# Two matmuls of 256 columns with the same weights become one of 512: the parts of x side by side

## The chip, the core and the metric

The kernel runs on one core of a Trainium2 chip. The engines of the core are named as in the profile: PE (TensorE, matmuls; PEld is its weight load), DVE (VectorE), ACT (ScalarE), POOL (GpSimd) and SP (SyncE, which issues most DMAs). The metric is the device time of one execution in microseconds.

## The reference

Two layers of a decoder on 256 tokens of width 2048, in float32. Layer 0 mixes by forgetting attention (8 heads of 128) beside a diagonal state-space part, layer 1 by sliding-window attention; each mixer is followed by a layer norm, and a gated feed-forward layer with a causal convolution of width 3 by another one.

```python
def _conv_ffn(x, w_up, conv_w, conv_b, w_down):
    s_len = x.shape[1]
    h = jnp.einsum('bsd,df->bsf', x, w_up)                 # 2048 -> 2 x 5504
    hp = jnp.pad(h, ((0, 0), (CONV_WIDTH - 1, 0), (0, 0)))
    h = conv_b + sum(conv_w[t] * hp[:, t:t + s_len] for t in range(CONV_WIDTH))
    gate = h[..., :D_FF]
    val = h[..., D_FF:]
    return jnp.einsum('bsf,fd->bsd', jax.nn.silu(gate) * val, w_down)
...
    proj = jnp.einsum('bsd,de->bse', x, w_in)              # layer 0: q, k, v, forget gate, u
    z = jnp.einsum('bsc,ce->bse', jax.nn.gelu(y.reshape(bsz, s_len, SSM_WIDTH)), w_glu)
    ssm = z[..., :SSM_WIDTH] * jax.nn.sigmoid(z[..., SSM_WIDTH:])
```

## The kernel before

Every float32 operand of a large product is split into two float32r parts, hi (ACT rounds it, L110 for weights) and lo (DVE subtracts, L115), and a product w x is built of three: hi(w) hi(x), hi(w) lo(x) and lo(w) hi(x). All matmuls go through `mm` (L234).

The weights stream through the kernel once, in the order of their use, in chunks of 512 KB (128 partitions x 1024 columns): `Stream` loads a chunk by SP into one of five raw buffers, splits it into one of four pairs of rotating buffers (tiles `hi` and `lo` in the profile) and hands it over. `done()` after a chunk frees its buffers, splits further chunks as far as three are held, and then pumps the side generators: each emits one step of other work (state-space vectors, an attention head, a finished column of the feed-forward layer). The order of all instructions on every engine is that in which this code emits them.

There are two shapes of product. In `amm` the stationary operand is 128 tokens of a transposed activation and 512 weight columns move: the result is natural, [token, feature]. It serves v, the output projections, the down projections and all of layer 1's mixer. In `bmm` the stationary operand is a 128 x 128 block of the weights, and the 256 tokens of the transposed x move: the result is [feature, token]. `xT[:, k]` holds k-tile k as [128, 2, 256], the hi part in index 0 of the second axis, the lo part in index 1. `bmm` serves u (the input of the state-space part, 8 tiles of 16 k-tiles), the forget gate, q and k of 8 heads (`b_tile`), the GLU, and columns 2 to 42 of both up projections, where a column j is a pair of 128 features, one of the gate and one of the value (`up_chunk`, four chunks to a pair). These are 3152 k-tiles, each with three matmuls into the first 256 columns of a PSUM bank of 512.

What reads the banks: ACT copies u to the tile `ut`, which goes through memory to the state-space part; ACT copies q (scaled) and k to the tiles `qk`, and one pump later the head's first product of q and k stands on PE. For the GLU, ACT takes the sigmoid of one bank and DVE multiplies it by the other. For the feed-forward layer `finish_gen` does ACT's scaling with bias from the bank, one pump later four DVE convolution steps from the bank, then silu and product, then the split into `act`.

Around a layer norm, `boundary` transposes x four tiles at a time (`turn`), through a scratch tile `x32`, by lists of steps (`PLAN_TAIL`, `PLAN_MID`, `PLAN_HEAD`).

Of the kernel before, what the change touches and what calls it, by code (L numbers as in the profile page):

```python
# [21 lines left out]
P = 128  # L22
T = 256
# [22 lines left out]
# around a layer norm, after each chunk: s split the next chunk (s0, s1: with the statistics of that half  # L46
# of the tokens in between), n normalize, t transpose, l second parts; digits: half, quarter of the columns
# [9 lines left out]
class Stream:  # L57
    """Weights in the order of use: DMA, split into two float32r parts, hand over. The parts of an item
    go to a rotating buffer, or to where its dst says: a function that gives (hi, lo), or None as long
    as there is no room."""  # L60
# [28 lines left out]
    def split_next(self, steps=None, late=False):  # L89
        """steps: a serial chain of short vector instructions to put in between; late: give back the  # L90
        function that does the second part"""
# [77 lines left out]
    def get(self):  # L169
        """The next chunk's parts; free() or done() must follow each, in order, after its last use."""  # L170
        while self.split <= self.pos:
            assert self.room(self.split, 0)
            self.split_next()
        o = self.outs.pop(self.pos)
        self.pos += 1
        return o
# [24 lines left out]
def trunk(ctx: ExitStack, tc: tile.TileContext, A, out):  # L201
# [39 lines left out]
    def k_exp(o, x, t, tk, ti):  # L241
        """o = exp(x); t, tk float scratch, ti int32 scratch. Yields the time of what it emitted."""
# [18 lines left out]
    def k_sincos(s, c, x, t, tk):  # L261
        """s, c = sin(x), cos(x)."""
# [28 lines left out]
    def gmul(o_re, o_im, a, b, t1, t2):  # L291
        """cmul on GpSimd, for the small tables it has time for"""
# [5 lines left out]
    def cmul(o_re, o_im, a, b, t1, t2):  # L298
        """(o_re, o_im) = a * b, complex; a, b are (re, im) pairs, the outputs no inputs."""
        mul(t1, a[0], b[0])  # L300
        mul(t2, a[1], b[1])
        sub(o_re, t1, t2)
        mul(t1, a[0], b[1])
        mul(t2, a[1], b[0])
        add(o_im, t1, t2)

# [26 lines left out]
    def ext(place, c):  # L333
        """the last four of the eight chunks on either side of a layer norm"""
# [71 lines left out]
    def warm(f):  # L406
        """the table of f, ahead of its first use"""
        S.activation(spare, spare, f)

# [1 line left out]
    def bmm(ps, hi, lo, k, first, last, src=None):  # L411
        """ps[f, t] += w[k, f] x[k, t]"""
        s = xT if src is None else src
        mm(ps, hi, s[:, k, 0, :], first, False)
        mm(ps, hi, s[:, k, 1, :], False, False)
        mm(ps, lo, s[:, k, 0, :], False, last)

    def amm(o, hi, lo, src, k, tb, first, last):
        """o[t, f] += x[k, t] w[k, f] for one half of the tokens"""
# [5 lines left out]
    def a_chunk(part, o, src, k, tb, first, last, n=2):  # L425
        """One chunk of the stream: n k-tiles of 512 columns."""
# [29 lines left out]
    def ln_stats(tb):  # L456
        """mean in lnw[:, tb, 0], 1 / sqrt(var + eps) in lnw[:, tb, 2], one short step at a time"""
# [20 lines left out]
    def four_places(t_, a=0):  # L478
        """room for the parts of four chunks in t_ [P, n, 2, T]"""
# [4 lines left out]
    def boundary(li, tail, resid, after_tail, head):  # L484
        """The last eight chunks of a product, the layer norm, the first eight chunks of the next
        product, each for one half of the tokens after the other: the norm of one half runs under the
        products of the other."""
        with tc.tile_pool(name="lnp", bufs=1) as lp:
# [5 lines left out]
            def turn(tb, q):  # L494
# [3 lines left out]
                x32 = mk(lp, [P, 4, P], tag="x32", bufs=3)  # L498
# [56 lines left out]
    def affine_gen(li, pool):  # L555
        """Gain and bias on the natural x, which only the next residual needs."""
# [18 lines left out]
    class Ffn:  # L575
# [13 lines left out]
        def up_chunk(self, part, c):  # L589
            hi, lo = part  # L590
            for kk in range(4):
                k = 4 * c + kk
                for e in range(2):
                    sl = slice(kk * T + e * P, kk * T + e * P + P)
                    bmm(self.ps[e][:, :T], hi[:, sl], lo[:, sl], k, k == 0, k == KT - 1)

        def head(self, part, tb, c):
            """columns 0 and 1 of the up projection, natural"""
# [17 lines left out]
        def finish(self, j):  # L616
            """convolution, gate and split of column j, among the next chunks"""
            self.gens.append(st.add(self.finish_gen(j, self.ps), 0.1))

        def finish_gen(self, j, ps):  # L620
            cw, y = self.cw, []
            for e in range(2):
# [17 lines left out]
        def run(self, li):  # L640
            """Everything but the last four chunks of the down projection."""
# [36 lines left out]
    def final(ffn, li):  # L678
        """The last layer norm, to the output."""
# [33 lines left out]
    def rope_gen(rp):  # L713
        """cos and sin of the rotary angles, and the sinks"""
# [12 lines left out]
    def apply_rope(t_, nh, rt_):  # L727
        """t_ [P, 2, nh, 64], in place on the first 16"""
# [166 lines left out]
    # =================================================================  # L895
    # layer 0, mixer
    # =================================================================
    cell = {}

    def s5_gen(p, wk, u4):  # L900
        """State-space part, everything but the u projection. Yields the vector work it emitted, in us;
        0 leaves the rest to the next call, for what waits on another engine."""
# [32 lines left out]
        def phasors():  # L935
            """Powers 0..7 of w = (cs + i sn)^4, in pb, and of w^8, in pa."""
# [65 lines left out]
        def tab(dst, sc, src, b):  # L1002
            """dst = sc * src, complex, in blocks on the diagonal of each pair of groups"""
# [577 lines left out]
```

## Time and profile before

| | before |
|---|---|
| median of 3 runs | 2156.82 us (2156.72 to 2157.05) |
| the profiled execution: its span | 2155.2 us |
| beside the span, to the median of the runs | 1.6 us |
| PE busy | 2123.6 us (99%), 14236 matmuls |
| DVE busy | 1380.7 us (64%) |
| ACT busy | 1056.6 us (49%) |
| DMA | 389.22 MB, mean 181 GB/s |

Busy time of PE is time in which at least one matmul is under way; durations of neighbouring matmuls overlap, so the distance between their starts, and not their duration, says how many fit into a stretch. The layer 0 mixer lasts until about 400 us, the feed-forward layer of layer 0 until about 1150 us, the mixer of layer 1 until about 1410 us, and the second feed-forward layer to the end.

### The profile page before, as it was taken

The numbers are of one execution on the slowest core, as the hardware profiler recorded it, in microseconds if no ns is written. First come the engines' busy times: TensorE is split into PE (matmuls) and PEld (weight loads), VectorE is DVE, ScalarE is ACT, GpSimd is POOL, SyncE is SP. The second block draws the span as 40 slices with busy tenths as digits, with TensorE's granted clock in tenths as the row PEclk, the third lists the DMA queues.
The fourth block names the chain that finished last, engine by engine and source line by source line (L and its number), as shares of the span: only waits on it lengthen the run. The fifth ranks groups of instructions, "written<-read, shape, count | busy, mean of one in ns | idle before, by whom it ended". The sixth has DMA issues, their size and how long they took to land.

```text
span 2155.2 us, 35663 instructions
## 1 busy us (share of the span) xinstructions
PE 2123.6 (99%) x14236; PEld 1934.8 (90%) x14236; DVE 1380.7 (64%) x2120; ACT 1056.6 (49%) x1586; POOL 78.1 (4%) x143
## 2 busy tenths in 40 slices
PE   8999999999999999999999999999999999999997
PEld 8899989799999999988887877889999999988886
DVE  7898856786566566544456876767656656654445
ACT  5445544655555455433336665465555545543332
POOL 4600000000000000000001000000000000000000
PEclk9999999999999999999999999999999999999999
DMA  8554456575665665656664644656665566656654
GB/s 289 153 168 130 128 193 203 163 217 185 186 182 181 186 184 180 186 183 187 190 200 147 186 127 127 205 160 210 183 186 182 181 186 185 179 186 189 189 183 160
DMA packets 111478, 389.22 MB, mean 181 GB/s; under 512 B 13072, under 2 KB 15120, under 8 KB 111056
## 3 DMA queue, kind: packets, MB, share of 16 engines
q1 hardware_dynamic: 104112, 371.37, 55.3%
q10 hardware_dynamic: 5712, 10.20, 1.7%
q0 software_dynamic: 1488, 5.38, 0.8%
q8 instruction: 112, 1.84, 0.3%
q14 instruction: 54, 0.44, 0.1%
HBM read 383.75 MB, written 3.15 MB: 180 GB/s over the span
## 4 chain that ended last, share of the span: by engine, by line
PE 96%; DVE 3%; ACT 1%; issue 1%; DMA 0%; DVEq 0%; ACTq 0%
PE bank L234 94%; DVE t L231 0%; DVE t L213 0%; PE bank L497 0%; DVE t L115 0%; DVE t L228 0%; PE bank L820 0%; PE bank L1031 0%; DVE z L213 0%; DVE lo L115 0%; ACT x L501 0%; DVE t L127 0%; DMA raw<-wu 0%; PE bank L823 0%; PE bank L779 0%
## 5 line engine op out<-in xcount | busy, mean ns | idle before, releaser
L115 DVE TENSOR_TENSOR lo<-raw,hi 128x1024 fp32r<-128x1024 f32 (+1 forms) x674 | 818.9, 1218 | 652.5 <-ACT hi L110 650.6
L234 PE MATMUL bank<-t,hi 128*128 128x256 f32 x6304 | 1140.2, 284 | 6.8 <-ACT t L110 6.0
L110 ACT CAST hi<-raw 128x1024 fp32r<-128x1024 f32 x677 | 705.7, 1045 | 688.1 <-PE bank L234 570.1
L234 PEld LDWEIGHTS bank<-t,hi 128*128 128x128 f32 x6304 | 985.1, 192 | 8.4 <-ACT t L110 6.0
L234 PE MATMUL bank<-t,lo 128*128 128x256 f32 x3152 | 893.0, 283 | 0.0
L234 PE MATMUL bank<-hi,t 128*128 128x512 f32 x2248 | 720.8, 397 | 0.0
L234 PEld LDWEIGHTS bank<-t,lo 128*128 128x128 f32 x3152 | 606.0, 192 | 0.1
L234 PEld LDWEIGHTS bank<-hi,t 128*128 128x128 f32 x2248 | 423.0, 188 | 102.2 <-issue 3.8
L234 PE MATMUL bank<-lo,t 128*128 128x512 f32 x1124 | 443.8, 395 | 0.4 <-DVE lo L115 0.4
L234 PEld LDWEIGHTS bank<-lo,t 128*128 128x128 f32 x1124 | 211.7, 188 | 49.5 <-DVE lo L115 1.3
L625 ACT ACTIVATE y<-bank,t 128x256 f32<-128x256 f32 x172 | 87.9, 562 | 134.1 <-PE bank L234 127.4
L231 DVE SCALAR_TENSOR_TENSOR y<-bank,t,y 128x255 f32<-128x255 f32 (+1 forms) x344 | 141.6, 475 | 1.9 <-ACT y L625 1.9
L234 PE MATMUL bank<-t,t 128*128 128x512 f32 (+3 forms) x422 | 89.6, 357 | 9.6 <-DVE t L115 7.8
L234 PEld LDWEIGHTS bank<-t,t 128*128 128x128 f32 (+1 forms) x422 | 63.0, 177 | 23.0 <-DVE t L115 8.8
L634 ACT ACTIVATE y<-y 128x256 f32<-128x256 f32 x86 | 35.9, 418 | 31.9 <-DVE y L231 31.9
L804 ACT ACTIVATE p<-bank,sm 128x128 f32<-128x128 f32 (+1 forms) x64 | 26.1, 420 | 45.2 <-DVE sm L213 45.2
L501 ACT ACTIVATE x<-bank,t 128x128 f32<-128x128 f32 x96 | 36.1, 457 | 19.5 <-PE bank L497 19.4
L213 DVE TENSOR_TENSOR t<-y,t 128x256 fp32r<-128x256 f32 x86 | 35.9, 419 | 0.9 <-ACT t L237 0.9
L213 DVE TENSOR_TENSOR y<-y,y 128x256 f32<-128x256 f32 x86 | 35.9, 420 | 0.3 <-ACT y L634 0.3
L237 ACT CAST t<-y 128x256 fp32r<-128x256 f32 x86 | 34.5, 402 | 3.3 <-DVE y L213 3.2
L213 DVE TENSOR_TENSOR t<-t,gbn 128x1024 f32<-128x1024 f32 x24 | 29.3, 1222 | 10.2 <-DMA gbn<-ln 10.2
L213 DVE TENSOR_TENSOR t<-bank,t 128x256 fp32r<-128x256 f32 (+3 forms) x34 | 17.6, 524 | 24.5 <-ACT t L237 24.4
(163 smaller groups left out, 899.0 us busy)
## 6 DMA issues: line engine op xcount, KB each, us to landing
raw<-wup SPq DMA_DIRECT2D x328, 512.0 KB, 3.6
raw<-wdn SPq DMA_DIRECT2D x168, 512.0 KB, 3.6
raw<-wo SPq DMA_DIRECT2D x64, 512.0 KB, 3.6
raw<-wi SPq DMA_DIRECT2D x40, 512.0 KB, 3.7
raw<-wqk SPq DMA_DIRECT2D x32, 512.0 KB, 3.6
raw<-wu SPq DMA_DIRECT2D x16, 512.0 KB, 5.5
raw<-wv SPq DMA_DIRECT2D x16, 512.0 KB, 3.7
raw<-wg SPq DMA_DIRECT2D x16, 512.0 KB, 4.0
```

Of the source, the lines that this page charges most:

```text
L110: self.nc.scalar.copy(hi, r)
L115: eng.tensor_tensor(lo, r, hi.bitcast(F32), op=ALU.subtract)
L213: V.tensor_tensor(o, a, b, op=op)
L231: V.scalar_tensor_tensor(o, a, s, b, op0=op0, op1=op1)
L234: PE.matmul(o, lhsT=l, rhs=r, start=start, stop=stop)
L237: S.copy(hi, src)
L501: S.activation(x32[:, j], pt[:, j * P:(j + 1) * P], AF.Identity, bias=lnT[:, li, 1, k:k + 1], scale=lnT[:, li, 0, k:k + 1])
L625: S.activation(y[e], ps[e][:, :T], AF.Identity, bias=cw[:, n, 3:4], scale=cw[:, n, 2:3])
L634: S.activation(y[0], y[0], AF.Silu)
L804: S.activation(pp[:, e], vv[:, e], AF.Exp, bias=sm[:, 0, qb, e:e + 1], scale=1.0, accum_out=sm[:, 2, qb, e:e + 1])
```

## The change

`bmm` issues two matmuls instead of three. The hi part of the weights multiplies both parts of the transposed x, 512 columns, into the whole bank: hi(w) hi(x) lands in columns 0 to 255, hi(w) lo(x) in 256 to 511. The lo part of the weights multiplies the hi part of x, 256 columns, into columns 256 to 511. Whoever reads the bank adds the halves: `joined` copies the second half out of PSUM on ACT and adds the first on DVE. The q tile is scaled by ACT on the way and added by one scaled step of DVE; the GLU joins both of its banks ahead of the sigmoid; `finish_gen` joins both banks of a pair into new tiles `h0` and `h1` one pump ahead of its old first step. Columns 0 and 1 of each up projection, which come from `amm`, are not joined. The scratch tile `x32` has two buffers instead of three. Comments are taken out, so line numbers move.

```diff
-    def bmm(ps, hi, lo, k, first, last, src=None):
-        s = xT if src is None else src
-        mm(ps, hi, s[:, k, 0, :], first, False)
-        mm(ps, hi, s[:, k, 1, :], False, False)
-        mm(ps, lo, s[:, k, 0, :], False, last)
+    def bmm(ps, hi, lo, k, first, last):
+        mm(ps, hi, xT[:, k].rearrange("p a t -> p (a t)"), first, False)
+        mm(ps[:, T:], lo, xT[:, k, 0, :], False, last)
+
+    def joined(o, ps, view=lambda a: a):
+        S.copy(o, view(ps[:, T:]))
+        add(o, o, view(ps[:, :T]))
...
-                x32 = mk(lp, [P, 4, P], tag="x32", bufs=3)
+                x32 = mk(lp, [P, 4, P], tag="x32", bufs=2)
...
-                    bmm(self.ps[e][:, :T], hi[:, sl], lo[:, sl], k, k == 0, k == KT - 1)
+                    bmm(self.ps[e], hi[:, sl], lo[:, sl], k, k == 0, k == KT - 1)
...
-            self.gens.append(st.add(self.finish_gen(j, self.ps), 0.1))
+            self.gens.append(st.add(self.finish_gen(j, self.ps, j >= 2), 0.1))
...
-        def finish_gen(self, j, ps):
+        def finish_gen(self, j, ps, halves):
             cw, y = self.cw, []
+            if halves:
+                h = [mk(self.w, [P, T], tag=f"h{e}", bufs=1) for e in range(2)]
+                for e in range(2):
+                    joined(h[e], ps[e])
+                ps = h
+                yield 0
...
-                    S.copy(ut, o.rearrange("p (n l) -> p l n", l=LCH))
+                    joined(ut, o, lambda a: a.rearrange("p (n l) -> p l n", l=LCH))
...
-    S.copy(ft, ps[0:8, :T])
+    joined(ft, ps[0:8])
...
             if j == 0:
-                S.mul(t_, ps[:, :T], 1.0 / math.sqrt(128.0))
+                c = 1.0 / math.sqrt(128.0)
+                S.mul(t_, ps[:, T:], c)
+                stt(t_, ps[:, :T], c, t_, ALU.mult, ALU.add)
             else:
-                S.copy(t_, ps[:, :T])
+                joined(t_, ps)
...
-        S.activation(sg, zz[1][:, :T], AF.Sigmoid)
-        mul(sg, sg, zz[0][:, :T])
+        joined(zl, zz[0])
+        joined(sg, zz[1])
+        S.activation(sg, sg, AF.Sigmoid)
+        mul(sg, sg, zl)
```

On PE the triples become pairs at every place alike. In an up projection (`t_77` is xT, the banks are those of a column pair) these rows stand before the change, where "x2" is two matmuls with the same weights, one after the other:

```order
L234 MATMUL bank_5771<-t_77,hi_5729 128x256 x2
L234 MATMUL bank_5771<-t_77,lo_5730 128x256
L234 MATMUL bank_5772<-t_77,hi_5729 128x256 x2
L234 MATMUL bank_5772<-t_77,lo_5730 128x256
L234 MATMUL bank_5771<-t_77,hi_5761 128x256 x2
```

and at the same place with the change:

```order
L234 MATMUL bank_5122<-t_77,hi_5084 128x512
L234 MATMUL bank_5122<-t_77,lo_5085 128x256
L234 MATMUL bank_5123<-t_77,hi_5084 128x512
L234 MATMUL bank_5123<-t_77,lo_5085 128x256
L234 MATMUL bank_5122<-t_77,hi_5108 128x512
```

The order of tiles and chunks is the same; the two matmuls with a hi block have become one of twice the columns.

On ACT, one column pair of an up projection, from the cast of the pair before (`t_4533`, after the change `t_4070`, is `act`) to the next cast of this kind; before:

```order
L237 CAST t_4533<-y_392_5329 128x256
L110 CAST hi_5470<-raw_5292 128x1024
L625 ACTIVATE y_400_5476<-bank_5332,t_4534 128x256
L625 ACTIVATE y_401_5478<-bank_5333,t_4534 128x256
L110 CAST hi_5511<-raw_5325 128x1024
L110 CAST hi_5549<-raw_5362 128x1024
L634 ACTIVATE y_400_5476<-y_400_5476 128x256
L110 CAST hi_5585<-raw_5403 128x1024
```

and with the change:

```order
L237 CAST t_4070<-y_421_4914 128x256
L418 COPY h_422_5008<-bank_4888 128x256
L418 COPY h_423_5009<-bank_4889 128x256
L110 CAST hi_5032<-raw_4873 128x1024
L634 ACTIVATE y_426_5038<-h_422_5008,t_4071 128x256
L634 ACTIVATE y_427_5040<-h_423_5009,t_4071 128x256
L110 CAST hi_5058<-raw_4910 128x1024
L110 CAST hi_5084<-raw_4940 128x1024
L643 ACTIVATE y_426_5038<-y_426_5038 128x256
L110 CAST hi_5108<-raw_4970 128x1024
L237 CAST t_4070<-y_427_5040 128x256
```

The copies are new; they now stand where PE's last matmul of the pair is waited for, and the activations come a chunk later and read the joined tiles.

On DVE, in the stretch of q and k of the fifth head (`z` and `ph` are state-space vectors, `fsm` and `fp` the head before), with the change:

```order
L213 TENSOR_TENSOR z_216_2210<-bank_2140,ph_1944 128x512
L231 SCALAR_TENSOR_TENSOR qk_220_2215<-bank_2105,qk_220_2215 128x256
L115 TENSOR_TENSOR lo_2236<-raw_1971,hi_2235 128x1024
...
L115 TENSOR_TENSOR lo_2264<-raw_2029,hi_2263 128x1024
L213 TENSOR_TENSOR z_216_2210<-z_216_2210,z_217_2211 128x512
L213 TENSOR_TENSOR z_218_2212<-z_218_2212,z_219_2213 128x512
L1136 SCALAR_TENSOR_TENSOR z_217_2211<-t_200,z_216_2210 128x512
L213 TENSOR_TENSOR qk_224_2278<-qk_224_2278,bank_2218 128x256
L115 TENSOR_TENSOR lo_2299<-raw_2086,hi_2298 128x1024
```

Before, DVE had no instruction that wrote q or k (tile `qk`). The step for q now stands behind one product of the state-space part, the one for k behind its first scan.

## Rows read from the trace of the kernel before

**Rows 1.** The page: span, busy time by engine, and the chain that ended last.
```profile
span 2155.2 us, 35663 instructions
PE 2123.6 (99%) x14236; PEld 1934.8 (90%) x14236; DVE 1380.7 (64%) x2120; ACT 1056.6 (49%) x1586; POOL 78.1 (4%) x143
...
PE 96%; DVE 3%; ACT 1%; issue 1%; DMA 0%; DVEq 0%; ACTq 0%
PE bank L234 94%; DVE t L231 0%; DVE t L213 0%; PE bank L497 0%; DVE t L115 0%; DVE t L228 0%; PE bank L820 0%; PE bank L1031 0%; DVE z L213 0%; DVE lo L115 0%; ACT x L501 0%; DVE t L127 0%; DMA raw<-wu 0%; PE bank L823 0%; PE bank L779 0%
```

**Rows 2.** Waits of PE, the two largest: us in total, times, longest.
```profile
PE bank L234 <- DVE t L115: 8.6, 4, 2.7
PE bank L234 <- ACT t L110: 6.0, 1, 6.0
```

**Rows 3.** Groups by shape of PE, whole span: busy us, mean ns of one.
```profile
L234 PE MATMUL bank<-t,hi 128*128 128x256 f32 x6304 | 1140.2, 284 | 6.8 <-ACT t L110 6.0 <-DVE t L115 0.8
L234 PE MATMUL bank<-t,lo 128*128 128x256 f32 x3152 | 893.0, 283 | 0.0
```

**Rows 4.** Windows, up projection: length, busy PE, PEld, DVE, ACT, POOL; clock, DMA.
```profile
600.00:700.00 100.00, 100.00 (x836) 100.00 (x835) 61.52 (x88) 50.63 (x70) 0.00 (x0) 1.00 0.60 184
```

**Rows 5.** Timeline of PE, up projection: start, length, merged matmuls.
```profile
800.12 0.40 PE L234 MATMUL bank<-t,hi 128*128 128x256 f32 x2
...
811.64 0.40 PE L234 MATMUL bank<-t,hi 128*128 128x256 f32 x2
```

**Rows 6.** Timeline of PE, output projection of layer 0, state-space half.
```profile
365.14 0.61 PE L234 MATMUL bank<-hi,t 128*128 128x512 f32 x2
...
372.62 0.61 PE L234 MATMUL bank<-hi,t 128*128 128x512 f32 x2
```

**Rows 7.** Timeline of PE, down projection of the first feed-forward layer.
```profile
904.20 0.63 PE L234 MATMUL bank<-hi,t 128*128 128x512 f32 x2
...
911.23 0.63 PE L234 MATMUL bank<-hi,t 128*128 128x512 f32 x2
```

**Rows 8.** Timeline of PE, scores of layer 1's attention (moving operand: its keys).
```profile
1203.15 0.51 PE L234 MATMUL bank<-t,qT 128*128 128x256 f32 x3
1203.50 0.28 PE L234 MATMUL bank<-t,t 128*128 128x256 f32 x1
1203.62 0.86 PE L234 MATMUL bank<-t,qT 128*128 128x512 f32 x3
1204.32 0.40 PE L234 MATMUL bank<-t,t 128*128 128x512 f32 x1
```

**Rows 9.** Groups by shape of ACT up to 440 us: the copy of k.
```profile
L1386 ACT COPY qk<-bank 128x256 f32<-128x256 f32 x8 | 3.1, 384 | 1.0 <-PE bank L234 1.0
```

**Rows 10.** Groups by shape of DVE up to 440 us: a product and a scaled step.
```profile
L213 DVE TENSOR_TENSOR sg<-sg,bank 128x256 f32<-128x256 f32 x8 | 3.4, 419 | 4.9 <-ACT sg L1432 4.9
L231 DVE SCALAR_TENSOR_TENSOR y<-bank,t,y 128x255 f32<-128x255 f32 x4 | 1.7, 476 | 0.0
```

**Rows 11.** Waits from 480 to 1000 us, the largest entry.
```profile
DVE lo L115 <- ACT hi L110: 208.3, 140, 2.5
```

**Rows 12.** Windows, 20 us in the stretch of q and k (columns as in rows 4).
```profile
200.00:220.00 20.00, 20.00 (x166) 19.84 (x165) 19.60 (x30) 9.30 (x18) 0.00 (x0) 1.00 0.51 148
```

**Rows 13.** Timelines of DVE and PE there: what precedes the products of heads five and six.
```profile
204.20 1.22 DVE L1127 TENSOR_TENSOR_SCAN z<-t,z 128x512 f32<-128x512 f32 x1
217.47 1.89 DVE L213 TENSOR_TENSOR z<-t,bt 128x512 f32<-128x512 f32 x3
...
206.20 0.39 PE L234 MATMUL bank<-qk,qk 128*128 128x128 f32 x2
219.80 0.39 PE L234 MATMUL bank<-qk,qk 128*128 128x128 f32 x2
```

**Rows 14.** Timeline of ACT, a sigmoid of the GLU with the idle time before it.
```profile
341.84 0.39 ACT L1432 ACTIVATE sg<-bank 128x256 f32<-128x256 f32 x1 [1.96 <-PE bank L234]
```

**Rows 15.** Timeline of PE, its second matmul of all.
```profile
7.36 0.58 PE L234 MATMUL bank<-t,hi 128*128 128x256 f32 x1 [0.76 <-DVE t L115]
```

More of the change, by code (lines that the diff above doesn't have):

```diff
@@ L1338, in trunk @@
                     st.get()
-                o = ps[i - i0][:, :T]
+                o = ps[i - i0]
                 for j in range(8):
@@ L1359, in trunk @@
     for k in range(KT):
-        bmm(ps[:, :T], hi[:, 8 * k:8 * k + P], lo[:, 8 * k:8 * k + P], k, k == 0, k == KT - 1)
+        bmm(ps, hi[:, 8 * k:8 * k + P], lo[:, 8 * k:8 * k + P], k, k == 0, k == KT - 1)
     st.done()
     ft = mk(fp, [8, T])
-    S.copy(ft, ps[0:8, :T])
+    joined(ft, ps[0:8])
     gate = st.add(fox_gate(ft, fp))
@@ L1380, in trunk @@
             ps = bank(acc)
-            b_tile(ps[:, :T], 2)
+            b_tile(ps, 2)
             t_ = mk(fp, [P, T], tag=f"qk{j}", bufs=2)
             if j == 0:
-                S.mul(t_, ps[:, :T], 1.0 / math.sqrt(128.0))
+                c = 1.0 / math.sqrt(128.0)
+                S.mul(t_, ps[:, T:], c)
+                stt(t_, ps[:, :T], c, t_, ALU.mult, ALU.add)
             else:
-                S.copy(t_, ps[:, :T])
+                joined(t_, ps)
             qk.append(t_)
@@ L1421, in trunk @@
             for k in ks:
-                bmm(z[c][:, :T], hi[:, k * P:(k + 1) * P], lo[:, k * P:(k + 1) * P], k, k == 0, k == 7)
+                bmm(z[c], hi[:, k * P:(k + 1) * P], lo[:, k * P:(k + 1) * P], k, k == 0, k == 7)
     for c in range(4):
@@ L1428, in trunk @@
             for j in range(2):
-                b_tile(z[j][:, :T], 1)
+                b_tile(z[j], 1)
         sg = mk(gp, [P, T], tag="sg")
+        zl = mk(gp, [P, T], tag="zl")
         zz = z[2 * i:2 * i + 2] if i < 2 else z
-        S.activation(sg, zz[1][:, :T], AF.Sigmoid)
-        mul(sg, sg, zz[0][:, :T])
+        joined(zl, zz[0])
+        joined(sg, zz[1])
+        S.activation(sg, sg, AF.Sigmoid)
+        mul(sg, sg, zl)
         split_to(xT[:, 8 + i, 0, :], xT[:, 8 + i, 1, :], sg)
```

## The prediction

> **What bounds the kernel now.** I read the page's head and its chain of waits first: PE is busy 2123.6 us of a span of 2155.2 us, and the chain that ended last runs through PE for 96% of the span, 94% on the matmul line L234 [rows 1]. Then the waits of PE: the two largest entries come to 8.6 and 6.0 us in five waits [rows 2], so there is next to no idle time to win; what counts is how long a matmul holds PE. The groups by shape name what the change touches: 6304 matmuls of 256 columns with the hi part of a weight as stationary operand and 3152 with the lo part [rows 3], that is 3152 triples hi, hi, lo. The windows say what the other engines do meanwhile: in the first up projection PE is busy without a gap, DVE 62% and ACT 51% of the time [rows 4].
>
> The number that matters is the pitch, the distance from start to start, for a duration in these rows holds latency that the next matmul overlaps. In the up projection 32 triples go from 800.12 to 811.64 us: 0.360 us each, 0.120 us per matmul of 256 columns [rows 5]. For 512 columns there are two paces. In the output projection of layer 0, where the operands are x^T and the rotating weight parts, 11 triples take 7.48 us: 0.680 us each, 0.2267 us per matmul [rows 6]. In the down projection, with the activations as one operand, 10 triples take 7.03 us: 0.703 us, 0.2343 us per matmul [rows 7]. Products of layer 1's attention give 0.2333 us (three in 0.70 us), and four matmuls of 256 columns just ahead of them 0.47 us, 0.1175 us each [rows 8].
>
> **The change, part by part.** *PE.* Each triple of 256 columns becomes one matmul of 512 and one of 256; the columns stay 768. The clock was granted in full there, the 2.4 GHz level [rows 4]. From 256 to 512 columns the faster pace grows by 0.1067 us, which is 256 periods of that clock: a column costs one period. Taken off, 0.0133 us per matmul is left at 256 columns [rows 5] as at 512 in the faster pace [rows 6], and 0.021 us in the slower [rows 7]. This fixed part is what a merged pair pays once instead of twice. For the 512 I take 0.2267, because there the operands lie in the same two buffers as in the merged product, x^T and the rotating parts, with the roles exchanged; the other end is 0.2343. For the 256 behind it I keep 0.120; the other end is 0.1175. The new pair is then 0.3467 us and saves 13.3 ns; the ends are 15.8 and 5.7 ns. Some ten triples run at the start before the clock is up, so 3140 x 13.3 ns = 41.9 us saved (ends 50 and 18 us).
>
> Here a rule of the notes speaks against the change. The Trainium skill, TensorE: Matmul & The Clock Gate, section "Back-to-back issue gap", puts the isolated pitch at N/2.4 + 2.5 ns, so that merging would save 2.5 ns, 7.9 us in all. The trace does not agree with its constant: its fixed part is 13 to 21 ns.
>
> *Feed-forward layers, 41 column pairs each.* Each pair gets two ACT copies out of PSUM (0.384 us each by the like copy of k) [rows 9] and two DVE additions with a PSUM operand (0.419 us) [rows 10]: 0.77 us of ACT and 0.84 us of DVE for a PE time of 32 x 0.3467 = 11.1 us. DVE goes from 0.62 x 11.52 = 7.1 us to 7.9 us, 72%; ACT from 5.8 to 6.6 us, 60%. I cost this at nothing: DVE's idle time there is a wait for the next cast (208.3 of 520 us) [rows 11], and the cast waits for a weight buffer that PE still reads, so splits run up to three chunks (8 us) ahead. If that cover went, the bare price is 2 x (0.384 + 0.419) = 1.6 us per pair. The banks come free at the join, two pumps earlier than the four convolution steps let them go; the convolution starts one pump later, and only the last pair of a layer could feel it, whose rows the down projection reads last in each of its column blocks. The later steps read SBUF instead of PSUM; I keep their price.
>
> *u, q and k, layer 0.* Here DVE also carries the state-space vectors: 19.60 us busy of 20 from 200 us on [rows 12]. Added: 8 joins of u, one of the gate, and for each of 8 heads a q step (0.476 us, as the like step) and a k step (0.419 us) [rows 10]: 9 x 0.419 + 8 x 0.895 = 10.9 us. Until now q and k needed ACT alone; now the head's product waits for DVE's queue. For the fifth head the k step stands behind the scan that starts at 204.20 and lasts 1.22 us, so it ends at 205.84, before the product at 206.20. For the sixth it stands behind three products from 217.47 to 219.36, ends at 219.78 or, pushed by the two steps before it less 0.4 us of slack, at 220.3: after the product's old start of 219.80 [rows 13]. So about 0.5 us at the worst heads, less where DVE has gaps. u's additions fall into chunks in which DVE waits for a cast anyway. I take 3 us for this stage (ends 0 and 10.9). The u vectors reach memory some 0.5 us later, long before they are used.
>
> *GLU.* Each pass gets two more copies and additions ahead of its sigmoid: copy, copy, addition, about 1.2 us longer, where ACT was idle 1.96 us before the sigmoid [rows 14]. Hidden, except for the first two passes, which come together: 0.5 us (ends 0 and 2.4).
>
> *Start.* The first matmul now needs both parts of x. PE ran one matmul early and then waited 0.76 us for the lo part [rows 15]; that early one is lost: 0.3 us, at most its 0.58 us.
>
> *x32 with two buffers instead of three.* Each transposition at a layer norm then needs the second part of the one two before it; the plan has that subtraction emitted by then in every case. Nothing; a late one would cost one subtraction, some 0.7 us, at three norms.
>
> Sum: -41.9 + 3 + 0.5 + 0.3 = -38.1 us on the span of 2155.2 us. The median of the runs, 2156.8 us, lies 1.6 us above the span; so 2118.7, given as **2119 us** (-1.8%).
>
> **The rivals.** (B) The merged matmul goes at the slower pace, 0.2343 us: 5.7 ns per triple, 17.9 us, less 3.8 us of costs: 2142.7 us. For it: most 512-column matmuls of this kernel run so, and I know no cause of the two paces. Against: the stretch with the operands in the same two buffers has the faster one throughout.
>
> (C) Columns are all that counts: the 512 takes as long as the two it replaces, 0.240 us. Nothing is saved and 3.8 us are added: 2160.6 us. It decides from 0.2388 us on (3.8 us / 3140 = 1.2 ns). Against it: no stretch that I read has more than 0.2343. By the page's constant named above, the same case ends at 2152.7 us.
>
> (D) Slower: the joins stop the queues of ACT and DVE in the up projection. The copy waits for PE to end its column; behind it stand the casts, behind the addition the subtractions of the next chunks. If the lead of three chunks is used up, each pair shows up to 1.6 us: 82 x 1.6 = 131 us, so up to 2118.7 + 131 = 2250 us. It turns the gain into a loss from 0.43 us per pair on (32 x 13.3 ns). For it: the addition now makes DVE wait for PE's last matmul of a pair, through ACT. Against it: ACT's old first step waited for that same matmul, and PE had no gap in that window [rows 4].
>
> **How the numbers follow.** My forecast 0.62, with a range of its own of 2108 to 2128 us (15.8 ns and costs near nothing; costs of 13 us); B 0.20; C 0.09; D 0.09. About 0.2%, 4.3 us, is what a measurement of this kernel can tell from no change. My forecast and B are faster by more: 0.82, and 0.01 of C joins them; 0.08 of C is within that bound, with 0.01 of D; 0.08 is slower. The range 2108 to 2147 us takes in my case and B with its costs up to 8 us, and leaves out C, D and the tails.
>
> **What would show it.** Right: PE with 3152 hi matmuls of 512 columns and as many lo of 256; pair pitch 0.347 us in the up projections and no PE gap there, DVE near 72% and ACT near 60%; an up projection shorter by 17.5 us a layer (41 x 0.427); a few PE waits on DVE, of up to 1 us, at the heads between 120 and 240 us. Wrong: a pair pitch of 0.354 (B) or 0.36 (C); PE waits on the subtraction of L115 or the cast of L110 between 450 and 900 us (D); DVE waits of several us ahead of each head's product, which would make the layer 0 mixer eat the gain.

## The result and the profile after

| | before | after |
|---|---|---|
| median of 4 runs each, same chip | 2156.94 us (2156.72 to 2157.28) | 2135.20 us (2134.24 to 2136.38) |
| ratio after to before | | 0.9902, 95% interval 0.9888 to 0.9916 |
| span of the profiled execution | 2155.2 us | 2134.0 us |

The change makes the kernel faster by 1.0%: 21.2 us of span, where 38.1 us were forecast. The head of the page and the chain that ended last, after:

```profile
span 2134.0 us, 29675 instructions
PE 2089.1 (98%) x11084; PEld 1759.7 (82%) x11084; DVE 1464.5 (69%) x2325; ACT 1110.9 (52%) x1766; POOL 74.7 (3%) x143
...
PE 90%; DVE 6%; ACT 2%; DMA 1%; issue 1%; POOL 0%; SPq 0%; ACTq 0%; DVEq 0%; POOLq 0%
```

PE has 3152 matmuls fewer and is busy for 34.5 us less, but the span fell by 21.2 us only: the chain, 96% PE before [rows 1], is now 90% PE and 6% DVE. The pace in an up projection is not the reason. PE's timeline there (start, length), 16 merged pairs from the first row to the last:

```profile
799.99 0.40 PE L234 MATMUL bank<-t,hi 128*128 128x512 f32 x1
800.22 0.28 PE L234 MATMUL bank<-t,lo 128*128 128x256 f32 x1
800.34 0.39 PE L234 MATMUL bank<-t,hi 128*128 128x512 f32 x1
...
805.53 0.40 PE L234 MATMUL bank<-t,hi 128*128 128x512 f32 x1
```

That is 5.54 us, 0.346 us a pair, against 0.360 us a triple [rows 5]. The windows say the same of the other engines (length, then busy PE, PEld, DVE, ACT, POOL, clock, DMA), first an up projection, then a stretch of layer 0's mixer:

```profile
600.00:700.00 100.00, 100.00 (x579) 87.49 (x578) 71.73 (x109) 58.30 (x91) 0.00 (x0) 1.00 0.61 191
60.00:80.00 20.00, 11.04 (x50) 8.16 (x49) 15.16 (x30) 6.02 (x9) 13.58 (x27) 0.94 0.52 150
```

In the up projection PE still has no gap and DVE is at 72%, ACT at 58%. From 60 to 80 us PE is busy 11.04 of 20 us; before, it was 18.82:

```profile
60.00:80.00 20.00, 18.82 (x124) 14.87 (x123) 18.54 (x34) 8.92 (x14) 19.04 (x32) 1.00 0.56 165
```

To see where the difference arises I put a mark where both programs do the same thing: the first transpositions of the first up projection (columns 0 and 1 of the feed-forward layer of layer 0). Their row on PE, before and after:

```profile
430.61 1.03 PE L613 MATMUL bank<-t,gbn 128*128 128x128 f32 x8
```
```profile
444.48 1.04 PE L616 MATMUL bank<-t,gbn 128*128 128x128 f32 x8
```

Up to this mark the changed kernel is 13.9 us late. Behind it, it needs 2134.0 - 444.5 = 1689.5 us where the kernel before needs 2155.2 - 430.6 = 1724.6: 35.1 us less, and 2 x 41 x 32 = 2624 pairs times the predicted 13.3 ns are 34.9 us. So the feed-forward layers paid in full, and the mixer of layer 0 took 13.9 us back. (In the other profiled runs with the up projections merged the stretch behind the mark takes 1689.5 to 1692.5 us, so the 35.1 us are known to some 3 us.)

What happens in that mixer is seen in the waits up to 440 us (who waited for what: us in total, times, longest). The first row has no counterpart before; PE's wait on the DVE `lo` came to 0.4 us in that stretch before:

```profile
ACT hi L110 <- DVE ut L213: 27.6, 7, 7.1
...
PE bank L234 <- DVE lo L115: 4.0, 6, 1.0
```

ACT's casts of weights (`hi`, L110) wait 27.6 us for DVE's addition to `ut`, on which they don't depend. ACT's timeline shows how (idle time before an instruction in brackets; ACTq is the issue of a DMA from ACT's queue):

```profile
48.97 0.37 ACT L418 COPY ut<-bank 128x256 f32<-128x256 f32 x1 [1.89 <-PE bank L234]
56.00 0.33 ACTq L1357 DMA_DIRECT2D t<-ut  x1
56.43 0.41 ACT L110 CAST hi<-raw 128x256 fp32r<-128x256 f32 x1 [7.08 <-DVE ut L213]
56.82 0.37 ACT L418 COPY ut<-bank 128x256 f32<-128x256 f32 x1
61.22 0.33 ACTq L1357 DMA_DIRECT2D t<-ut  x1
61.64 1.05 ACT L110 CAST hi<-raw 128x1024 fp32r<-128x1024 f32 x1 [4.45 <-DVE ut L213]
```

and DVE meanwhile:

```profile
48.98 1.26 DVE L115 TENSOR_TENSOR lo<-raw,hi 128x1024 fp32r<-128x1024 f32 x1
...
51.24 1.22 DVE L115 TENSOR_TENSOR lo<-raw,hi 128x1024 fp32r<-128x1024 f32 x1
...
55.56 0.41 DVE L213 TENSOR_TENSOR ut<-ut,bank 128x256 f32<-128x256 f32 x1
56.87 0.43 DVE L115 TENSOR_TENSOR lo<-raw,hi 128x256 fp32r<-128x256 f32 x1 [0.89 <-ACT hi L110]
```

The copy of u's second half ends at 49.3 us. The DMA that takes `ut` to memory, the next thing in ACT's queue, cannot be issued before DVE has added the first half, and the addition stands on DVE behind two subtractions and the state-space vectors of that pump: 55.56 us. Only after the issue, at 56.00, does the next cast run, and then DVE waits for that cast in turn. In the kernel before, the same issue followed ACT's own copy at once, and the same cast came 0.8 us after the copy's start instead of 7.5:

```profile
47.15 0.37 ACT L1347 COPY ut<-bank 128x256 f32<-128x256 f32 x1 [1.95 <-PE bank L234]
47.55 0.33 ACTq L1348 DMA_DIRECT2D t<-ut  x1
47.98 0.41 ACT L110 CAST hi<-raw 128x256 fp32r<-128x256 f32 x1 [0.45 <-DVE t L226]
```

So some 0.45 us of each of the seven waits is the issue itself, as before; the rest is new. The eighth store holds other casts (L398), for 2.6 us.

How this reaches PE is seen in its three longest waits between 60 and 80 us, none of which is there before, and in what DVE and POOL did just ahead of them:

```profile
66.70 0.50 PE L234 MATMUL bank<-hi,t 128*128 128x512 f32 x1 [1.27 <-DVE ut L213]
76.17 0.29 PE L1232 MATMUL bank<-t,t 8*128 8x8 f32 x2 [3.67 <-DVE t L213]
78.70 1.94 PE L1040 MATMUL bank<-t,t 128*128 128x128 f32 x8 [2.24 <-POOL t L295]
```
```profile
75.71 0.40 DVE L213 TENSOR_TENSOR t<-t,bank 8x256 f32<-8x256 f32 x1
```
```profile
74.41 2.33 POOL L1336 DMA_DIRECT2D u<-t  x4 [2.47 <-DMA t<-ut]
...
77.94 0.73 POOL L295 TENSOR_TENSOR t<-t,t 128x32 f32<-128x32 f32 x1
```

DVE is late because of the late casts, and PE waits 3.67 us for the addition that joins the halves of the forget gate (75.71 us). POOL loads u back from memory; it waited 2.47 us for the late store to land, and the table for which PE then waits 2.24 us stands behind these loads.

The Trainium skill, PSUM — Partial Sum Buffer, section "Engine vs sequencer instructions", says that "ScalarE/VectorE/GpSimdE queues are strict FIFO". The 27.6 us agree with it: here a DMA's issue kept its place in that order too.

### The profile page after: what moved, and what is told of

It reads as the page before. It is cut to its first block, busy times and chain, and to the rows that moved or that the text cites. A ratio compares the mean times of both kernels' runs of the same rounds, so it can differ in the third digit from the quotient of the medians.

```text
span 2134.0 us, 29675 instructions
## 1 busy us (share of the span) xinstructions
PE 2089.1 (98%) x11084; PEld 1759.7 (82%) x11084; DVE 1464.5 (69%) x2325; ACT 1110.9 (52%) x1766; POOL 74.7 (3%) x143
## 4 chain that ended last, share of the span: by engine, by line
PE 90%; DVE 6%; ACT 2%; DMA 1%; issue 1%; POOL 0%; SPq 0%; ACTq 0%; DVEq 0%; POOLq 0%
PE bank L234 88%; DVE lo L115 2%; DVE t L213 1%; DVE t L231 1%; DVE z L213 1%; ACT hi L110 1%; DMA raw<-wu 1%; DVE t L228 1%; DMA t<-x 0%; PE bank L1040 0%; PE bank L500 0%; DVE t L115 0%; PE bank L829 0%; ACT x L504 0%; DVE t L127 0%
## 5 line engine op out<-in xcount | busy, mean ns | idle before, releaser
L115 DVE TENSOR_TENSOR lo<-raw,hi 128x1024 fp32r<-128x1024 f32 (+1 forms) x674 | 819.0, 1219 | 526.8 <-ACT hi L110 525.5
L234 PE MATMUL bank<-t,hi 128*128 128x512 f32 x3152 | 1101.0, 395 | 7.5 <-DVE t L115 7.5
L110 ACT CAST hi<-raw 128x1024 fp32r<-128x1024 f32 x677 | 705.1, 1047 | 651.3 <-PE bank L234 566.0
L234 PE MATMUL bank<-t,lo 128*128 128x256 f32 x3152 | 877.5, 278 | 1.8 <-DVE lo L115 1.8
L234 PEld LDWEIGHTS bank<-t,hi 128*128 128x128 f32 x3152 | 592.7, 188 | 145.5 <-DVE t L115 7.5
L234 PEld LDWEIGHTS bank<-t,lo 128*128 128x128 f32 x3152 | 593.8, 188 | 3.2 <-DVE lo L115 3.0
L231 DVE SCALAR_TENSOR_TENSOR y<-h,t,y 128x255 f32<-128x255 f32 (+1 forms) x328 | 136.4, 478 | 0.5 <-ACT y L634 0.5
L418 ACT COPY h<-bank 128x256 f32<-128x256 f32 x164 | 60.2, 373 | 87.5 <-PE bank L234 85.0
L634 ACT ACTIVATE y<-h,t 128x256 f32<-128x256 f32 x164 | 89.9, 597 | 15.2 <-DVE h L213 15.1
L213 DVE TENSOR_TENSOR h<-h,bank 128x256 f32<-128x256 f32 x164 | 66.9, 421 | 21.2 <-ACT h L418 21.2
```

The costliest lines, as they stand in the source:

```text
L110: self.nc.scalar.copy(hi, r)
L115: eng.tensor_tensor(lo, r, hi.bitcast(F32), op=ALU.subtract)
L213: V.tensor_tensor(o, a, b, op=op)
L231: V.scalar_tensor_tensor(o, a, s, b, op0=op0, op1=op1)
L234: PE.matmul(o, lhsT=l, rhs=r, start=start, stop=stop)
L418: S.copy(o, view(ps[:, T:]))
```

## The experiments

The theory (Q below): the issue of u's store holds ACT's queue, and with it the casts, until DVE has added. The main rival (W): DVE has more work in a stretch where it was busy anyway, and it is the added work that costs.

**u as before.** The first experiment takes u out of the change: three matmuls, one plain copy; all else stays merged. The product of its 128 k-tiles loses its forecast gain of 1.7 us.

```diff
-                    bmm(o, hi[:, j * P:(j + 1) * P], ...)
+                    bmm3(o[:, :T], hi[:, j * P:(j + 1) * P], ...)
...
-                    joined(ut, o, lambda a: a.rearrange("p (n l) -> p l n", l=LCH))
+                    S.copy(ut, o[:, :T].rearrange("p (n l) -> p l n", l=LCH))
```

> The u product alone goes back to three matmuls of 256 columns and a plain ACT copy; all else is the changed kernel. Theory Q: the DMA that stores u is issued by ACT and waits for DVE's addition, so ACT's queue, casts and all, stands still (27.6 us of waits in the changed kernel), and this delays the whole layer 0 mixer. Then the first up projection starts near 429 us instead of 444.5, and the time is 2119 to 2121 us; u's own gain on PE, 128 x 13.3 ns = 1.7 us, is given up. Rival W: the added DVE work as such (18 us in the layer 0 mixer) is what delays it; u's share of it is a fifth, so about 4 us come back: 2131 us.

Measured: 2122.29 us (2120.52 to 2125.51), ratio to before 0.9838 (0.9825 to 0.9852). The first up projection starts at 430.89 us, and no cast waits for an addition to `ut`. The time is 1.3 us over the expected stretch; the mark comes 13.6 us earlier than in the whole change, as Q has it. But the experiment takes away the wait and the work together, so it does not yet rule W out.

**Another queue for the store.** u stays merged, the DMA is issued by POOL.

```diff
-                    S.dma_start(out=ud[P * i:P * i + P], in_=ut)
+                    G.dma_start(out=ud[P * i:P * i + P], in_=ut)
```

> The changed kernel with one word changed: the DMA that stores u is issued by POOL instead of ACT. DVE does the same work. Theory Q: ACT's casts no longer stand behind the wait; 2117 to 2121 us, if POOL, which also builds state-space tables, is not held up in turn. Rival W: nothing in DVE's work changes, 2135 us.

Measured: 2128.36 us (2126.06 to 2130.49), ratio 0.9868 (0.9855 to 0.9882); first up projection at 437.77 us. Half of the loss is gone, not all, and the time is 7 us over the expected stretch, which was to hold if POOL is not held up in turn. The waits up to 440 us and the timelines of POOL and ACT show why:

```profile
POOL t L1357 <- DVE ut L213: 20.9, 2, 19.0
```
```profile
56.42 0.62 POOL L1357 DMA_DIRECT2D t<-ut  x1 [0.17 <-DVE t L213]
```
```profile
59.45 0.37 ACT L418 COPY ut<-bank 128x256 f32<-128x256 f32 x1 [9.25 <-DMA t<-ut]
```

Now POOL stands for DVE in the first two stores. Later ones are queued behind the state-space tables that POOL computes, from 44.8 us almost without a break: the fifth is issued at 56.42 us. `ut` has two buffers, so the copy of a later u on ACT waits for that store to land: 9.25 us. The held queue had moved, and reached ACT again through the buffer.

**Only the up projections merged.** Everything in layer 0's mixer is as before: u, gate, q, k, GLU.

```diff
-        bmm(ps, hi[:, 8 * k:8 * k + P], lo[:, 8 * k:8 * k + P], k, k == 0, k == KT - 1)
+        bmm3(ps[:, :T], hi[:, 8 * k:8 * k + P], lo[:, 8 * k:8 * k + P], k, k == 0, k == KT - 1)
...
-                joined(t_, ps)
+                S.copy(t_, ps[:, :T])
...
-        joined(zl, zz[0])
-        joined(sg, zz[1])
-        S.activation(sg, sg, AF.Sigmoid)
-        mul(sg, sg, zl)
+        S.activation(sg, zz[1][:, :T], AF.Sigmoid)
+        mul(sg, sg, zz[0][:, :T])
```

> Only the up projections use the merged matmul; u, gate, q, k and GLU are as before the change. By the pitch in the two traces (0.360 against 0.3463 us, 2624 pairs) it gains 35 to 36 us on the kernel before: 2121 to 2122 us. Against e1 it says what merging gate, q, k and GLU is worth: their PE gain is 400 x 13.3 ns = 5.3 us; theory Q leaves most of it (e1 2 to 3 us below this run), rival W eats it (e1 not below, or above).

Measured: 2122.96 us (2120.82 to 2124.09), ratio 0.9842 (0.9829 to 0.9856); first up projection at 431.69 us and 1689.6 us from there to the end. The feed-forward layers alone give the 35 us. The run with u as before, which has gate, q, k and GLU merged on top, lies 0.7 us below this one and not the 2 to 3 us that Q was to leave: for these parts the outcome is the one of W, and their merged k-tiles add nothing that can be measured.

**The joins of the feed-forward layers twice.** The changed kernel with each join of a column pair done a second time into the same tile.

```diff
                 for e in range(2):
                     joined(h[e], ps[e])
+                for e in range(2):
+                    joined(h[e], ps[e])
```

> The changed kernel with each join of the up projections done twice (the same copy and addition again), 164 more ACT copies and DVE additions of 0.37 and 0.42 us: DVE goes to about 79%, ACT to 65% there. If the joins are covered by PE, as the prediction costs them: no change, within 2 us of 2135. If they are at the edge (the prediction's rival D): up to 1.6 us for each of 82 column pairs, up to 131 us more.

Measured: 2139.78 us (2136.53 to 2144.83), ratio 0.9923 (0.9906 to 0.9940). The interval overlaps that of the changed kernel, but the median is 4.6 us above it, more than the expected 2. Only one of the four runs, the second shortest, has a profile, with a span of 2135.4 us against 2134.0. Its window of the up projection:

```profile
600.00:700.00 100.00, 100.00 (x579) 88.19 (x578) 78.53 (x127) 64.95 (x109) 0.00 (x0) 1.00 0.63 190
```

DVE rises to 79%, ACT to 65%, and PE has no gap still. At 1.6 us a pair in the open, 82 pairs would have cost 131 us; the second joins cost some 5 us at most, so nearly all of them are covered. Where the longer runs lost their time is not shown.

**The store one chunk later.** This parts Q from W. All work of the change is kept; only the DMA's issue moves behind the next chunk's casts in ACT's queue.

```diff
                 st.done()
+                stores()
                 if c == 1:
...
-                    S.dma_start(out=ud[P * i:P * i + P], in_=ut)
-                    if i % 2 == 1:
-                        load_u4(i // 2)
+                    held.append((i, ut))
```

`stores()` issues what `held` has, and `load_u4` after every second one.

> u stays merged and joined on ACT and DVE, all work of the changed kernel is kept; only the issue of the DMA that stores u moves behind the steps of the next chunk on ACT's queue, when the addition has long been done. Theory Q (the issue holds ACT's queue until DVE's addition, and the casts behind it come late): no wait of a cast on the addition to ut is left, the first up projection starts near 431 us as with u as before (444.5 in the changed kernel), time 2119 to 2123 us. Rival W (the eight additions themselves, in DVE's queue ahead of the second parts, are the cost): the first up projection still starts at 440 us or later, time 2131 us or more.

Measured: 2123.48 us (2123.13 to 2124.89), ratio 0.9848 (0.9835 to 0.9862). The mark on PE, and ACT's timeline:

```profile
430.70 1.04 PE L616 MATMUL bank<-t,gbn 128*128 128x128 f32 x8
```
```profile
50.77 1.05 ACT L110 CAST hi<-raw 128x1024 fp32r<-128x1024 f32 x1
54.01 0.33 ACTq L1345 DMA_DIRECT2D t<-ut  x1
54.43 0.37 ACT L418 COPY ut<-bank 128x256 f32<-128x256 f32 x1 [2.61 <-DVE ut L213]
54.70 1.05 ACT L110 CAST hi<-raw 128x1024 fp32r<-128x1024 f32 x1
```

The issue still waits up to 2.6 us, but what stands behind it is the next copy of u, not a cast that DVE needs. The casts' own wait for an addition is not quite gone, as was expected, but is down from 27.6 us to a single one of 1.6. The time is 0.5 us over the expected stretch; the mark is back at 430.70 us, with every addition still there: for u, W falls. The run takes away two things at once, the late casts and the late stores (the last one is issued at 61.00 us instead of 71.31), so the share of each in the loss is not shown.

**The wait without the change.** And the other way round: u exactly as before on PE, a plain copy, but a step of DVE that multiplies `ut` by 1.0 between the copy and the store.

```diff
                     S.copy(ut, o[:, :T].rearrange("p (n l) -> p l n", l=LCH))
+                    V.tensor_scalar(ut, ut, 1.0, None, op0=ALU.mult)
                     S.dma_start(out=ud[P * i:P * i + P], in_=ut)
```

> u as in the kernel before (three matmuls of 256 columns, a plain copy on ACT), the rest merged, but one step of DVE (ut times 1.0, in place) between the copy and the DMA that stores ut. Theory Q: the issue on ACT waits for DVE again, so the casts behind it come late as in the changed kernel: waits of casts on the step of ut of some 20 us or more, first up projection near 444 us, time near 2135 us, though PE does u exactly as before. Rival W (only the work counts): eight steps of at most 0.4 us, 3 us, so the first up projection near 434 us and 2125 us.

Measured: 2133.86 us (2133.10 to 2134.74), ratio 0.9895 (0.9882 to 0.9909). The mark and the wait:

```profile
442.71 1.04 PE L621 MATMUL bank<-t,gbn 128*128 128x128 f32 x8
```
```profile
ACT hi L110 <- DVE ut L1362: 27.5, 7, 6.7
```

The same seven waits, 27.5 us against 27.6, and nearly the same loss, without the merged product. The run differs from u as before by this one step, and its mark comes 11.8 us later: one step of DVE ahead of a store that ACT issues is enough.

**q and k as before.** With the store one chunk later, q and k as three matmuls and a plain copy.

```diff
-            b_tile(ps, 2)
+            b_tile(ps[:, :T], 2, bmm3)
...
-                joined(t_, ps)
+                S.copy(t_, ps[:, :T])
```

> As with the store one chunk later, but the products of q and k as three matmuls of 256 columns with a plain copy each. The merged q and k save 256 x 13.3 ns = 3.4 us of PE and add 16 steps of DVE (7.2 us), where DVE is busy nearly all the time. If DVE's waits eat the gain (the prediction's term of 3 us for this stage), this kernel is within 1.5 us of the one with the store one chunk later; if DVE has room, it is some 3.4 us longer; if the added steps cost their whole price, it is some 4 us shorter.

Measured: 2122.36 us (2120.91 to 2124.01), ratio 0.9843 (0.9829 to 0.9856); the mark at 430.51 us. Within 1.2 us of the kernel with them merged, the first of the three cases: the gain on PE is gone again. That DVE's waits are what eats it is shown only in part (see the rest of the mixer, below).

**Up projections, q and k merged; u, gate and GLU as before.**

```diff
-            b_tile(ps[:, :T], 2)
+            b_tile(ps, 2, bmm)
...
-                S.copy(t_, ps[:, :T])
+                joined(t_, ps)
```

(against the kernel with the up projections alone)

> Up projections, q and k merged; u, gate and GLU as three matmuls of 256 columns with one plain read each. By the stages of the earlier runs: to the first turn of the state-space tables 67.1 to 67.3 us, to the second 60.2 more (61.2 wherever the gate was joined), to the end of the heads 153.1 more (154.1 with q and k as before), to the first up projection 149.2 to 150.2 more, so 430 to 431 us there, and 2119.5 to 2121 us in all, the shortest so far by a microsecond or two, which the runs may not tell apart. Rival: the gain of one stage is taken back by the next as with q and k as before, and nothing is left of it: 2122 us.

Measured: 2122.39 us (2120.35 to 2124.50), ratio 0.9845 (0.9831 to 0.9858), the mark at 430.25 us, the span 2120.1 us. The trace goes by the expected stages, but the time is 1.4 us over the expected stretch, near the rival's 2122 us, and the runs do not tell this version from the others near 2122 to 2123 us.

**Two buffers for `x32`, alone.** The kernel before with that one line of the change.

```diff
-                x32 = mk(lp, [P, 4, P], tag="x32", bufs=3)
+                x32 = mk(lp, [P, 4, P], tag="x32", bufs=2)
```

> The kernel before with one thing of the change, two buffers for the transposed tokens at a layer norm instead of three. The prediction has this at nothing: the same time as before within 1 us, the waits of PE at the three norms as before. Rival: the transpositions wait for the second part of the one two before, some 0.7 us a time at three norms, 2 us or more longer.

Measured: 2157.29 us (2154.66 to 2159.28) beside 2156.20 us, ratio 1.0004 (0.9995 to 1.0013). The same, as far as runs that differ by 4 us can tell. The wait that the rival names is in the trace once: ACT waits 1.2 us for a subtraction ahead of a write of `x32`. PE's waits on L115 are the 8.6 us in four places of [rows 2], and the profiled span is 2155.8 us against 2155.2.

The stages of the mixer in all of these, by the starts of four groups of transpositions on PE (the state-space tables' first and second, the way back of the first state-space result behind the heads, and the mark), in us of each profiled execution:

| | first turn | to the second | to the way back | to the mark | mark | rest |
|---|---|---|---|---|---|---|
| before | 67.08 | 60.21 | 154.09 | 149.23 | 430.61 | 1724.6 |
| after | 78.70 | 62.85 | 153.14 | 149.79 | 444.48 | 1689.5 |
| u as before | 67.35 | 61.19 | 153.15 | 149.20 | 430.89 | 1692.5 |
| store on POOL | 70.36 | 65.18 | 153.06 | 149.17 | 437.77 | 1689.5 |
| up projections only | 67.25 | 60.19 | 154.09 | 150.16 | 431.69 | 1689.6 |
| joins twice | 78.52 | 62.70 | 153.15 | 150.04 | 444.41 | 1691.0 |
| store one chunk later | 67.13 | 61.16 | 153.14 | 149.27 | 430.70 | 1691.1 |
| u as before, DVE step | 77.79 | 62.52 | 153.13 | 149.27 | 442.71 | 1689.7 |
| later, q and k as before | 67.53 | 61.22 | 154.09 | 147.67 | 430.51 | 1689.8 |
| up projections, q, k | 67.52 | 60.12 | 153.07 | 149.54 | 430.25 | 1689.9 |
| before, two buffers for `x32` | 67.37 | 60.15 | 154.07 | 149.60 | 431.19 | 1724.6 |

## Why the prediction was right and where it was not

**The time lies in the stated range by luck.** 2135.20 us is inside 2108 to 2147 us, but outside the 2108 to 2128 us of the forecast itself. The range reached so far up to take in rival B, and B fell. What filled its place is a cost that the prediction did not have.

**The gain of PE held as a sum.** A pair takes 0.346 us, predicted 0.3467, so rivals B (0.354) and C (0.36) fall. Its parts are not those of the forecast. Averaged over the first feed-forward layer, the trace has 0.232 us from the start of the 512 columns to the start of the 256 behind them, and 0.115 us from there to the next 512 (the rows at 800 us show it: 0.23 and 0.12). The prediction took 0.2267 and 0.120. So the faster pace, taken because the operands lie in the same two buffers [rows 6], is not what these rows show; 0.232 is nearer to B's 0.2343, and a shorter 256 makes up for it. Whether the 256 columns are really faster there, or only their start is recorded later, the trace cannot tell. The Trainium skill, TensorE: Matmul & The Clock Gate, section "Back-to-back issue gap", gives N/2.4 + 2.5 ns as the gap of an isolated matmul, by which merging would save an estimated 2.5 ns. The trace has 0.360 - 0.346 = 14 ns a pair in a stream, and does not agree.

**The feed-forward layers held.** 35.1 us measured against 34.9; DVE 72% and ACT 58% against 72% and 60%; PE has no gap, and rival D falls with the joins done twice.

**The term of u failed.** The prediction had "u's additions fall into chunks in which DVE waits for a cast anyway" and "The u vectors reach memory some 0.5 us later, long before they are used", with 3 us for u, q and k and 10.9 us at most. It counted the addition, but not the DMA that follows it in the same queue as the casts. The wait of ACT is not DVE's 0.41 us but all that DVE has in its queue ahead of the addition, up to 7.08 us, and the stores went out late, not by 0.5 us: the last one was issued at 56.19 us before and at 71.31 us after. Nor was that long before u is used: POOL's loads stood waiting for it. The share of this one place is the distance of the two marks with and without it: 444.48 - 430.70 = 13.8 us. Most of it is there by the first turn (78.70 against 67.13 us).

**Part of the loss lies where the clock was low.** PE did nothing from 73 to 76 us, waiting for the addition that joins the forget gate, and the granted clock was 0.50 from 78 to 84 us. The windows (the clock is the third number from the end) and PE's timeline, after:

```profile
73.00:76.00 3.00, 0.00 (x0) 0.00 (x0) 3.00 (x5) 1.88 (x2) 1.59 (x3) 1.00 0.40 103
...
82.00:84.00 2.00, 2.00 (x6) 1.52 (x6) 1.93 (x5) 0.20 (x1) 1.92 (x3) 0.50 0.62 240
```
```profile
82.14 0.63 PE L234 MATMUL bank<-lo,t 128*128 128x512 f32 x1
82.57 1.05 PE L234 MATMUL bank<-hi,t 128*128 128x512 f32 x2
```

A granted clock of 0.50 is the 1.2 GHz level, and 512 columns then take 0.43 us, from 82.14 to 82.57, instead of some 0.23. With the store one chunk later the windows from 60 to 140 us have a clock of 1.00, and the stage behind the first turn is 1.7 us shorter (61.16 against 62.85 us).

**The rest of the mixer gave nothing.** 528 merged k-tiles were to gain 7.0 us there and to cost 3.8. With the hold gone the mark stands at 430.70 us, where it was: the 7.0 us are not to be seen. The windows up to the mark and of the heads (from the second turn to the way back), before and with the store one chunk later:

```profile
0.00:430.61 430.61, 416.81 (x2976) 379.16 (x2977) 329.91 (x574) 221.64 (x366) 69.27 (x140) 1.00 0.56 178
127.29:281.38 154.09, 153.63 (x1297) 146.31 (x1296) 126.27 (x197) 80.10 (x156) 4.27 (x8) 1.00 0.48 154
```
```profile
0.00:430.70 430.70, 412.89 (x2440) 349.63 (x2441) 342.33 (x615) 225.25 (x382) 68.78 (x140) 1.00 0.56 178
128.29:281.43 153.14, 151.75 (x1057) 133.28 (x1055) 131.86 (x213) 79.96 (x156) 4.28 (x8) 1.00 0.48 154
```

PE is idle for 17.8 us up to the mark, 13.8 before: 4.0 us of new waits (0.6 of them at the start, where the prediction had 0.3). And PE's busy time fell by 3.9 us only, not by 7.0. Three places can be read. The first turn comes at the same time with u merged, since PE ends up waiting 1.07 us for a state-space table from POOL there (its wait `PE bank L1040 <- POOL t L295`), which sets that point. In all three versions with the gate merged and the hold gone, the next stage takes 1.0 us more (61.2 against 60.2). The heads gain 1.0 of 3.4 us (153.1 against 154.1). Of the 2.4 us that are missing there, 0.9 is idle time of PE (1.39 against 0.46 us), most of it one wait, at the sixth head, for which the prediction had worked out 0.5 us:

```profile
220.09 0.49 PE L234 MATMUL bank<-qk,qk 128*128 128x128 f32 x2 [0.79 <-DVE qk L213]
```

Another 1.1 us is in the pace: averaged from one hi to the next, the trace has 0.357 us a pair in this stretch against 0.366 a triple, 9 ns instead of 13.3. Why it is less here is open. The prediction's own sign of a mixer that eats the gain, waits of several us ahead of each head's product, did not appear. The last stage gives back or takes away a microsecond or so without regard to the GLU; what sets it was not tried further.

So the sum, repaired: -35.1 us behind the mark; ahead of it -7.0 us of PE as forecast, +7.1 us that are missing again with the hold gone (4.0 of waits, 3.1 of gain that PE's busy time does not show), +13.8 us for the hold: -21.2 us, the measured one.

**x32** cost nothing that the runs can tell in the kernel before; in the changed kernel it was not tried alone, and the one wait of 1.2 us is there too.

## What to carry to other kernels

Before a plain copy becomes a copy on one engine and an addition on another, look at what stands behind it in the first engine's queue: in this kernel a DMA issued from there waited in order for the second engine, and held all that followed, casts that had nothing to do with it. Price such a step by the queue ahead of it on the second engine (7 us), not by its own length (0.4 us). Issue the transfer later, behind the work that others wait for; moving it to another busy queue shifts the wait and can bring it back through the buffers.

The best versions are, within what the runs can tell, equal at 2122 to 2123 us (-1.5 to -1.6%): the store one chunk later, u as before, or the up projections alone, which is the smallest change.

## What the runs showed of the hardware

- 512 columns and 256 behind them take 0.346 us in one stream, 14 ns less than three times 256 (0.360 us). From start to start 512 columns take 0.2267 us in the output projection, 0.2343 us in the down projection [rows 6, 7] and 0.232 us ahead of 256; why, stays open.
- A step of 0.41 us on DVE, behind others in DVE's queue, held ACT's casts for up to 7.08 us, seven times for 27.6 us in all, through the issue of a DMA.
- Reading the convolution's input from SBUF instead of PSUM did not make it faster. The groups, after (mean ns of one behind the busy time):

```profile
L231 DVE SCALAR_TENSOR_TENSOR y<-h,t,y 128x255 f32<-128x255 f32 (+1 forms) x328 | 136.4, 478 | 0.5 <-ACT y L634 0.5
...
L634 ACT ACTIVATE y<-h,t 128x256 f32<-128x256 f32 x164 | 89.9, 597 | 15.2 <-DVE h L213 15.1
```

The same step of DVE took 476 ns from PSUM [rows 10], and ACT's, before, was the shorter one:

```profile
L625 ACT ACTIVATE y<-bank,t 128x256 f32<-128x256 f32 x172 | 87.9, 562 | 134.1 <-PE bank L234 127.4
```

- At the start of the kernel before, matmuls went at about half pace while the profile gives a granted clock of 1.00. Six triples, between these two rows, take 3.84 us, 0.64 us each:

```profile
7.95 0.63 PE L234 MATMUL bank<-t,hi 128*128 128x256 f32 x2
...
11.79 0.63 PE L234 MATMUL bank<-t,hi 128*128 128x256 f32 x2
```
```profile
8.00:10.00 2.00, 2.00 (x11) 2.00 (x11) 1.17 (x3) 1.25 (x2) 0.81 (x2) 1.00 1.01 412
```

The prediction put this down to the clock ("before the clock is up"), which the granted clock does not show.
